# Opening of a pooling mixer and gated ConvFFN kernel: scale rows loaded and spread in four pieces, matmuls and averages of the first two tiles in another order, edge rows on another DMA queue

## The chip, the cores and the metric

The kernel runs on one core of one Trainium2 chip. The metric is device microseconds of the whole execution, as the median of three runs. All times below are in microseconds (us).

## What is computed

One layer of a decoder trunk: RMS norm, a causal pooling mixer with four windows, a residual, a second RMS norm, a gated ConvFFN (1024 to 2 x 2816 and back), a residual. The input is 1 x 1024 x 1024 in float32.

```python
h = rms_norm(x, norm_mix_g)
# pool_mixer: four groups of 256 channels, windows 2, 4, 8, 16
    groups.append(window_sum / count - xf[..., group])
d = jnp.stack(groups, axis=2)
y = einsum('bsgc,gcd->bsgd', d, w).reshape(bsz, seq, D_MODEL) + b
x = x + scale * y
f = conv_ffn(rms_norm(x, norm_ffn_g), ffn_w_in, ffn_conv_w, ffn_conv_b, ffn_w_out)
x = x + f
```

## The kernel before

The 1024 rows are cut into eight tiles `x0` to `x7` of 128 rows. For each tile the mixer makes these steps. `stat(j)` takes the mean square of a row (ScalarE, Square with a running sum, then Sqrt) and VectorE makes a factor of it. `mixer_norm(j)` multiplies the pooling band by that factor (VectorE, tile `bandr`). `mixer_window(j)` applies the band (TensorE, PSUM `psd`), and ScalarE copies the result to `dh`. `mixer_out(j)` multiplies by the pool weights (TensorE, PSUM `psy`, then two matmuls that add the bias rows), and VectorE adds the residual. `ffn_operand` transposes (PSUM `pst`) for the ConvFFN, whose two large products (names `X`, `Y`, `Z` and `oP`) fill the rest of the program after the first 60 us.

Ahead of that stands a short opening. Seven matmuls on a tile of zeros (`keep_warm`, L130) run while the first loads are on their way. The row of output scales (`rows`, 4 KB) is loaded into partition 0 of `rows_raw`, whose other 127 partitions are zeroed first by two memsets (L107 on VectorE, L108 on GpSimd). Two matmuls with a matrix of ones (`scale_rows`, L195) then spread that row to all partitions in PSUM `ps_scale`, and eight VectorE steps (`mixer_weights`, L200) multiply it and the norm's gain into the pool weights `wps`. `gain_rows` (L221) spreads the second norm's gain in the same way with the identity matrix, `pool_bias` prepares the bias rows. The last 16 rows of each tile are needed by the next one: they are loaded once for all tiles as `x_edge`, normed into `edge_band` (`edge_norm`) and multiplied in `mixer_edges` (PSUM `ps_edges`).

Each engine runs its instructions in order. That order is the order of the code with the constraints of `tc.issue_after`, which keep a block from being placed before a marked instruction. Loads stand in order on the queue of the engine that issues them: SyncE (SP) for nearly all, ScalarE for the scale row, GpSimd (POOL) for the eight-partition copy of the rows. PSUM for the mixer has three double banks (`bank2`) which the tiles `idle_ps`, `psd`, `ps_gain`, `psy`, `ps_edges`, `pst` take in turn.

Of the kernel before, what the change touches and what calls it, by code (L numbers as in the profile page):

```python
# [7 lines left out]
F32 = mybir.dt.float32  # L8
# [3 lines left out]
ALU = mybir.AluOpType  # L12
PSUM = bass.MemoryType.PSUM

P = 128
# [6 lines left out]
NG = 4  # L22
GRP = D // NG
WINDOWS = (2, 4, 8, 16)
HALO = 16
# [10 lines left out]
E0 = FAC + 2 * NG * HALO  # L36
# [7 lines left out]
NH = 512  # L44
# [4 lines left out]
def trunk_kernel(ctx: ExitStack, tc: tile.TileContext, x, consts, par, rows, pool_w, w_in, w_out, out):  # L49
    nc = tc.nc  # L50
# [11 lines left out]
    pp = pre.enter_context(tc.tile_pool(name="pre", bufs=1))  # L62
    ps_p = pre.enter_context(tc.tile_pool(name="ps_p", bufs=3, space=PSUM))

    def bank2(name):
        return ps_p.tile([P, 2 * NH], F32, tag="ps", name=name)

    def raw_tile(name):
        return work.tile([P, 2, D], F32, tag="raw", name=name, bufs=2)
# [15 lines left out]
    def load_x(j):  # L85
        if j < 2 or j >= 2 + XBUFS:
            xs[j] = hls.tile([P, D], F32, tag="hl", name=f"x{j}", bufs=7)
        else:
            xs[j] = pp.tile([P, D], F32, tag="x", name=f"x{j}", bufs=XBUFS)
        nc.sync.dma_start(xs[j], x[j * P : (j + 1) * P, :])  # L90

    cst = pp.tile([P, BD], F32, tag="cst", name="cst")
    band = pp.tile([P, NG, P], F32, tag="band", name="band")
    x_edge = work.tile([P, D], F32, tag="ha", name="x_edge", bufs=1)
    edge_band = work.tile([P, NG, P], F32, tag="sum", name="edge_band", bufs=3)
    def affine(t, src, op, fill, base, pattern, step):
        nc.gpsimd.affine_select(out=t, in_=src, compare_op=op, fill=fill, base=base, pattern=pattern, channel_multiplier=step)

    rows_raw = raw_tile("rows_raw")
    scale = rows_raw[:, 0, :]  # L100
    rows8, bias8 = (rows_raw[:NK, 1, i * NH : i * NH + 2 * P].rearrange("k (r p) -> k r p", p=P) for i in range(2))
    bias8 = bias8.bitcast(F32R)
    idle = work.tile([P, NH], BF16, tag="sum", name="idle", bufs=3)
    nc.vector.memset(idle, 0.0)
    eps_t = const.tile([P, 1], F32, tag="eps", name="eps_t")
    nc.vector.memset(eps_t, D * EPS)
    nc.vector.memset(scale[:, :NH], 0.0)  # L107
    nc.gpsimd.memset(scale[:, NH:], 0.0)  # L108
    warm = pp.tile([P, 1], F32, tag="warm", name="warm")
    with tc.issue_after(nc.scalar.dma_start(scale[:1, :], rows[:1, :]).ins):  # L110
        nc.scalar.activation(warm, eps_t, AF.Sqrt)

    nc.gpsimd.dma_start(rows8, rows.rearrange("r (k p) -> k r p", p=P))
    bias_hl = pp.tile([P, D], F32R, tag="bias_hl", name="bias_hl")
    nc.gpsimd.memset(bias_hl.bitcast(F32), 0.0)
    for g, w in enumerate(WINDOWS):
# [17 lines left out]
    nc.sync.dma_start(cst[:, :E0], consts[:, :E0])  # L134
    load_x(1)
    nc.sync.dma_start(par_sb[:, GM:], par[:, GM:])
    for g in range(0, NG, 2):
        nc.sync.dma_start(wp_raw[:, 2 * g : 2 * g + 4, :], pool_w[g : g + 2].rearrange("g (k p) d -> p (g k) d", p=P))
    nc.sync.dma_start(cst[:, E0:], consts[:, E0:])

    nc.sync.dma_start(x_edge, x.rearrange("(j r) d -> r j d", r=P)[P - HALO :, :, :])
    load_x(2)

    band0 = cst[:, :FAC].bitcast(BF16).rearrange("p (g s) -> p g s", s=P)
    fac = cst[:, FAC:E0].rearrange("p (c t) -> p c t", t=HALO)
# [3 lines left out]
    marks = {}  # L149

    def rstd_of(src, name):
        junk = pp.tile([P, D], BF16, tag="junk", name=f"junk_{name}")
        st = pp.tile([P, 4], F32, tag="st", name=f"st_{name}", bufs=8)
        nc.scalar.activation(junk, src, AF.Square, accum_out=st[:, 0:1])
        marks[name] = nc.scalar.activation(st[:, 1:2], st[:, 0:1], AF.Sqrt, bias=eps_t).ins
        nc.vector.tensor_scalar(st[:, 0:1], st[:, 0:1], D * EPS, None, op0=ALU.add)

        nc.vector.scalar_tensor_tensor(st[:, 3:4], st[:, 1:2], st[:, 1:2], st[:, 0:1], op0=ALU.mult, op1=ALU.add)
        nc.vector.reciprocal(st[:, 2:3], st[:, 3:4])
        return st[:, 1:2], st[:, 2:3]  # L160

    def normed(out, src, r):
        return nc.vector.tensor_scalar(out, src, r[0], r[1], op0=ALU.mult, op1=ALU.mult).ins
# [3 lines left out]
    def edge_norm():  # L167
        marks["edge"] = normed(edge_band, band_e, rstd_of(x_edge, "e"))

    def mixer_norm(j):  # L170
        t = bands[j] = pp.tile([P, NG, P], F32, tag="bandr", name=f"bandr{j}", bufs=2)
        marks[f"band{j}"] = normed(t, band if j else band0, stats[j])

    def windows(ps, src, weights):
        for c in range(NK):
            m = nc.tensor.matmul(ps[:, c * P : (c + 1) * P], src[:, c * P : (c + 1) * P], weights[:, c // 2, :], start=True, stop=True)  # L176
        return m.ins

    ones = pp.tile([P, P], F32R, tag="ones", name="ones")
# [3 lines left out]
    def mixer_edges():  # L183
        ps = marks["ps_edges"] = bank2("ps_edges")
        marks["edges_pe"] = windows(ps, x_edge, edge_band)
        first_edges()
        marks["edges"] = nc.scalar.activation(edges, ps.rearrange("p (c s) -> p c s", c=NK), AF.Copy).ins


    wps = pp.tile([P, 2 * NG, GRP], F32, tag="wps", name="wps")  # L190
    def scale_rows():

        ps = [ps_x.tile([P, NH], F32, tag="X", name=f"ps_scale{h}") for h in range(2)]
        for h in range(2):
            marks["scale"] = nc.tensor.matmul(ps[h], ones.bitcast(F32), scale[:, h * NH : (h + 1) * NH], start=True, stop=True).ins  # L195
        return [ps[g // 2][:, g % 2 * GRP : (g % 2 + 1) * GRP] for g in range(NG)]

    def mixer_weights(scale_b, chunks):
        for c in chunks:
            marks["wps"] = nc.vector.scalar_tensor_tensor(  # L200
                wps[:, c, :], scale_b[c // 2], par_sb[:, GM + c : GM + c + 1], wp_raw[:, c, :], op0=ALU.mult, op1=ALU.mult
            ).ins
# [14 lines left out]
    def gain_rows():  # L217
        ps = bank2("ps_gain")
        for k in range(NK):
            gain = par_sb[:, GF + k : GF + k + 1].to_broadcast([P, P])  # L220
            marks["gain_pe"] = nc.tensor.matmul(ps[:, k * P : (k + 1) * P], gain, ident, start=True, stop=True).ins  # L221
        gain_b = pp.tile([P, D], F32, tag="gain_b", name="gain_b")
        marks["gain"] = nc.scalar.activation(gain_b, ps, AF.Copy, scale=FOLD).ins
        return gain_b

    ds, gains = {}, []

    def mixer_window(j):
        ps = bank2(f"psd{j}")
        marks[f"psd{j}"] = windows(ps, xs[j], bands.pop(j))  # L230
        dh = ds[j] = pp.tile([P, NK, P], F32, tag="dh", name=f"dh{j}", bufs=2)
        ps3 = ps.rearrange("p (c s) -> p c s", c=NK)
        first = ps3[:, :, :HALO]
        if j == 0:
            marks["first"] = nc.vector.tensor_tensor(first, first, fac, ALU.mult).ins
        elif j > 1:
            nc.vector.tensor_tensor(first, first, edges[:, :, j * HALO : (j + 1) * HALO], ALU.add)
        marks[f"dh{j}"] = nc.scalar.activation(dh, ps3, AF.Copy).ins
# [208 lines left out]
    def stat(j):  # L447
        if j in xs and j not in stats:
            stats[j] = rstd_of(xs[j], f"a{j}")

    scale_b = scale_rows()
    stat(0)
    mixer_norm(0)
    with tc.issue_after(marks["band0"]):
        nc.vector.tensor_tensor(b8, b8, rows8[:, 0, :], ALU.mult)
        stat(1)
        mixer_norm(1)
    with tc.issue_after(marks["scale"]), tc.issue_after(marks["band1"]), tc.issue_after(marks["a1"]):
        mixer_window(0)
    with tc.issue_after(marks["dh0"]), tc.issue_after(marks["first"]):  # L460
        pool_bias()
    with tc.issue_after(marks["first"]):
        mixer_weights(scale_b, range(2 * NG))
    with tc.issue_after(marks["psd0"]), tc.issue_after(marks["dh0"]):
        mixer_window(1)
    with tc.issue_after(marks["dh1"]), tc.issue_after(marks["wps"]):
        edge_norm()
    with tc.issue_after(marks["e"]), tc.issue_after(marks["edge"]):
        stat(2)
        mixer_norm(2)  # L470
    with tc.issue_after(marks["psd1"]), tc.issue_after(marks["a2"]):
        gains.append(gain_rows())
    with tc.issue_after(marks["gain_pe"]), tc.issue_after(marks["band2"]):
        mixer_out(0, stats=False)
    with tc.issue_after(marks["psy0"]):
        mixer_edges()
    with tc.issue_after(marks["dh1+"]), tc.issue_after(marks["gain"]):
        stat(3)
        mixer_norm(3)
    with tc.issue_after(marks["band3"]), tc.issue_after(marks["edges"]):  # L480
        mixer_out_stats(0)
# [180 lines left out]
    for k in range(-SLOOK, len(oevents)):  # L662
# [9 lines left out]
        with tc.issue_after(lasts[-1]) if lasts else nullcontext():  # L672
            room = 4
            if k + OLOOK < len(oevents):
                e = oevents[k + OLOOK]
# [19 lines left out]
        if f == 0 and opens:  # L695
            for i in range(4):
                tag = ("XXYY" if set_ == "X" else "YZZZ")[i]
# [14 lines left out]
        for i, g, c, bank in steps:  # L712
            a, b = oops[p, g]
            alone = opens and (p, i) != ("P4", 3)
            for m, (u, v) in enumerate(((0, 0), (0, 1), (1, 0))):
                first = g == (NP2 - TAIL if c.start else 0) and m == 0
                nc.tensor.matmul(  # L717
                    bank, a[:, u, i * P : (i + 1) * P], b[:, v, c],
                    start=opens and first, stop=g == NP2 - 1 and m == 2, skip_group_check=not alone,
# [82 lines left out]
```

## Time and profile before

| | us |
|---|---|
| median of three runs | 701.74 (701.55 to 701.88) |
| the profiled execution | 702.16 |
| its span, first to last instruction | 700.3 |
| TensorE busy in it | 692.7 (99%) |
| VectorE busy | 598.9 (86%) |
| ScalarE busy | 343.3 (49%) |
| GpSimd busy | 13.2 (2%) |

The profile lists, for each engine, when an instruction started, how long it took and what ended the idle time before it. The chain of waits follows the work that ended last back to the start: what stands in it sets the end of the program.

### The profile page before, as it was taken

Reading aid. Unit: us, or ns where it says so; the run is one execution under the profiler, and the core shown is the slowest. Engines: PE = TensorE matmul, PEld = TensorE weight load, DVE = VectorE, ACT = ScalarE, POOL = GpSimd, SP = SyncE. Lnnn points to the kernel's source line nnn. Section 1 sums busy time; section 2 is a strip of 40 time slices with the busy share of each in tenths; the row PEclk is TensorE's granted clock in tenths of the full one; section 3 lists DMA queues with packets and bytes.
Section 4 is the critical chain, followed back from the end, with each engine's and each line's share of the span. In section 5 each row is a group of like instructions: output and inputs, shape, how many; then the busy total and the mean of one; then the engine's idle time right before and its main releaser. Section 6 shows DMA issues by size and latency. Waiting matters only on the chain.

```text
span 700.3 us, 8502 instructions
## 1 busy us (share of the span) xinstructions
PE 692.7 (99%) x3160; PEld 574.4 (82%) x3160; DVE 598.9 (86%) x884; ACT 343.3 (49%) x515; POOL 13.2 (2%) x31
## 2 busy tenths in 40 slices
PE   8999999999999999999999999999999999999998
PEld 5998778888888888888888888888888888888886
DVE  4788999999888888888988888876887988999985
ACT  5786645454444454444445454454554344444431
POOL 3021000000000000000000000000000000000000
PEclk9999999999999999999999999999999999999999
DMA  8974112222122112222222212229989700122131
GB/s 243 318 175 136 61 60 91 100 111 91 77 74 85 52 75 90 91 90 91 91 90 91 90 61 91 94 84 345 321 312 347 266 23 0 61 90 89 62 107 61
DMA packets 32556, 85.49 MB, mean 122 GB/s; under 512 B 3689, under 2 KB 5377, under 8 KB 29698
## 3 DMA queue, kind: packets, MB, share of 16 engines
q1 hardware_dynamic: 31328, 82.83, 33.4%
q0 software_dynamic: 1184, 2.11, 1.7%
q8 instruction: 25, 0.41, 0.2%
q14 instruction: 17, 0.14, 0.1%
q10 hardware_dynamic: 2, 0.00, 0.0%
HBM read 62.89 MB, written 19.92 MB: 118 GB/s over the span
## 4 chain that ended last, share of the span: by engine, by line
PE 97%; DVE 1%; DMA 1%; ACT 0%; issue 0%; DVEq 0%; ACTq 0%
PE oP L717 30%; PE Y L366 26%; PE Z L366 17%; PE X L366 16%; PE psy L253 4%; PE psd L176 2%; PE pst L286 1%; DMA rows_raw<-in_rows_dram 1%; PE psy L256 1%; PE ps_scale L195 0%; DVE n2f L317 0%; DVE T L306 0%; PE ps_gain L221 0%; PE ps_edges L176 0%; DVE n L271 0%; DVE S4s L77 0%
## 5 line engine op out<-in xcount | busy, mean ns | idle before, releaser
L717 PE MATMUL oP<-oBP,oAP 128*128 128x512 f32 (+1 forms) x924 | 208.8, 388 | 0.0
L717 PEld LDWEIGHTS oP<-oBP,oAP 128*128 128x128 f32 x924 | 172.9, 188 | 36.0 <-DVE oBP L77 0.3
L366 PE MATMUL Z<-T,S1s 128*128 128x512 f32 x264 | 64.1, 390 | 1.4 <-ACT T L305 1.2
L366 PE MATMUL X<-B,A11s 128*128 128x512 f32 x264 | 64.3, 390 | 0.0
L366 PE MATMUL Y<-T,S2s 128*128 128x512 f32 x264 | 64.0, 390 | 0.0
L366 PE MATMUL X<-B,A12s 128*128 128x512 f32 x264 | 63.5, 389 | 0.0
L366 PE MATMUL Y<-T,S3s 128*128 128x512 f32 x264 | 63.4, 389 | 0.0
L366 PE MATMUL Y<-T,A22s 128*128 128x512 f32 x264 | 63.4, 389 | 0.0
L366 PE MATMUL Z<-B,S4s 128*128 128x512 f32 x264 | 63.2, 389 | 0.0
L366 PEld LDWEIGHTS Z<-T,S1s 128*128 128x128 f32 x264 | 49.3, 188 | 12.6 <-ACT T L305 1.6
L366 PEld LDWEIGHTS Y<-T,S2s 128*128 128x128 f32 x264 | 49.4, 188 | 10.8 <-ACT S2s L76 0.4
L366 PEld LDWEIGHTS Y<-T,S3s 128*128 128x128 f32 x264 | 49.5, 188 | 10.3
L366 PEld LDWEIGHTS Y<-T,A22s 128*128 128x128 f32 x264 | 49.6, 188 | 10.3
L366 PEld LDWEIGHTS Z<-B,S4s 128*128 128x128 f32 x264 | 49.5, 188 | 10.3
L366 PEld LDWEIGHTS X<-B,A12s 128*128 128x128 f32 x264 | 49.5, 188 | 10.2
L366 PEld LDWEIGHTS X<-B,A11s 128*128 128x128 f32 x264 | 49.4, 188 | 10.2
L76 ACT ACTIVATE oBP<-blk 128x512 fp32r<-128x512 f32 x53 | 33.5, 633 | 49.1 <-PE oP L717 33.6
L77 DVE TENSOR_TENSOR oBP<-blk,oBP 128x512 fp32r<-128x512 f32 x53 | 36.7, 692 | 13.3 <-ACT oBP L76 13.3
L424 ACT ACTIVATE gate<-gate 128x1024 f32<-128x1024 f32 x22 | 23.3, 1061 | 44.5 <-DVE gate L415 44.5
L76 ACT ACTIVATE oAP<-blk 128x512 fp32r<-128x512 f32 x55 | 34.1, 621 | 19.2 <-DVE blk L317 15.9
L320 DVE TENSOR_TENSOR win<-win 128x512 f32<-128x512 f32 x60 | 41.3, 689 | 1.1
L77 DVE TENSOR_TENSOR oAP<-blk,oAP 128x512 fp32r<-128x512 f32 x55 | 37.8, 687 | 2.6 <-ACT oAP L76 2.6
(128 smaller groups left out, 940.8 us busy)
## 6 DMA issues: line engine op xcount, KB each, us to landing
win<-in_w_in_dram SPq DMA_DIRECT2D x22, 1024.0 KB, 4.8
g_dram<-val SPq DMA_DIRECT2D x22, 512.0 KB, 2.6
blk<-g_dram SPq DMA_DIRECT2D x33, 256.0 KB, 5.3
blk<-in_w_out_dram SPq DMA_DIRECT2D x31, 256.0 KB, 5.8
A12s<-g_dram SPq DMA_DIRECT2D x22, 256.0 KB, 5.2
B21s<-in_w_out_dram SPq DMA_DIRECT2D x22, 256.0 KB, 2.7
x<-in_x_dram SPq DMA_DIRECT2D x8, 512.0 KB, 4.9
x_dram<-x SPq DMA_DIRECT2D x8, 512.0 KB, 3.0
```

The costliest lines, as they stand in the source:

```text
L76: nc.scalar.activation(t[:, 0, :], src, AF.Copy)
L77: m = nc.vector.tensor_tensor(t[:, 1, :], src, t[:, 0, :].bitcast(F32), ALU.subtract)
L176: m = nc.tensor.matmul(ps[:, c * P : (c + 1) * P], src[:, c * P : (c + 1) * P], weights[:, c // 2, :], start=True, stop=True)
L253: nc.tensor.matmul(o, dh[:, c, :], wps[:, c, :], start=c % 4 == 0, stop=False, skip_group_check=True)
L256: m = nc.tensor.matmul(ps[:, cols], ones, bias_hl[:, cols], start=False, stop=True, skip_group_check=True)
L286: nc.tensor.transpose(ps[:, c * P : (c + 1) * P], n2[:, c * P : (c + 1) * P], ident)
L320: nc.vector.tensor_tensor(out, a, b, ALU.add)
L366: nc.tensor.matmul(bank, a[:, i, ks], b[:, l, k, :], start=opens and m == 0, stop=m == 11, skip_group_check=not opens)
L424: nc.scalar.activation(gate, gate, AF.Silu)
L717: nc.tensor.matmul(bank, a[:, u, i * P : (i + 1) * P], b[:, v, c], start=opens and first, stop=g == NP2 - 1 and m == 2, skip_group_check=n ...
```

## The change

The scale row goes as four pieces of 256 into four partitions of a tile with 256 columns; one VectorE memset zeroes these columns. A new tile `pick` (128 x 4, ones on its diagonal, made by GpSimd) takes the place of the matrix of ones: column g, stretched over 128 columns, selects row g, so there are four matmuls of 256 columns where two of 512 stood. The memset of the zeros for `keep_warm` goes from VectorE to GpSimd. On SP's queue the second part of the constants (identity and edge band) goes ahead of the pool weights, and `x_edge` leaves it for GpSimd's queue, so `x2` follows the pool weights. `gain_rows` goes between the windows of tiles 0 and 1, `stat(2)` ahead of the copy of tile 1, `edge_norm` behind it.

```diff
-    scale = rows_raw[:, 0, :]
+    scale = rows_raw[:, 0, :GRP]
...
-    nc.vector.memset(idle, 0.0)
+    nc.gpsimd.memset(idle, 0.0)
+    nc.vector.memset(scale, 0.0)
...
-    nc.vector.memset(scale[:, :NH], 0.0)
-    nc.gpsimd.memset(scale[:, NH:], 0.0)
...
-    with tc.issue_after(nc.scalar.dma_start(scale[:1, :], rows[:1, :]).ins):
+    with tc.issue_after(nc.scalar.dma_start(scale[:NG, :], rows[0].rearrange("(g d) -> g d", d=GRP)).ins):
...
+    pick = pp.tile([P, NG], F32, tag="pick", name="pick")
+    nc.gpsimd.memset(pick, 0.0)
+    affine(pick, pick, ALU.not_equal, 1.0, 0, [[1, NG]], -1)
...
+    nc.sync.dma_start(cst[:, E0:], consts[:, E0:])
     for g in range(0, NG, 2):
         nc.sync.dma_start(wp_raw[:, 2 * g : 2 * g + 4, :], pool_w[g : g + 2].rearrange("g (k p) d -> p (g k) d", p=P))
-    nc.sync.dma_start(cst[:, E0:], consts[:, E0:])
-
-    nc.sync.dma_start(x_edge, x.rearrange("(j r) d -> r j d", r=P)[P - HALO :, :, :])
     load_x(2)
+
+    nc.gpsimd.dma_start(x_edge, x.rearrange("(j r) d -> r j d", r=P)[P - HALO :, :, :])
...
-        for h in range(2):
-            marks["scale"] = nc.tensor.matmul(ps[h], ones.bitcast(F32), scale[:, h * NH : (h + 1) * NH], start=True, stop=True).ins
+        for g in range(NG):
+            marks["scale"] = nc.tensor.matmul(rows_b[g], pick[:, g : g + 1].to_broadcast([P, P]), scale, start=True, stop=True).ins
...
-    with tc.issue_after(marks["scale"]), tc.issue_after(marks["band1"]), tc.issue_after(marks["a1"]):
+    with tc.issue_after(marks["scale"]), tc.issue_after(marks["a1"]):
         mixer_window(0)
+    with tc.issue_after(marks["first"]):
+        mixer_norm(1)
...
+    with tc.issue_after(marks["psd0"]), tc.issue_after(marks["bias"]):
+        gains.append(gain_rows())
+    with tc.issue_after(marks["gain"]), tc.issue_after(marks["wps"]):
         stat(2)
         mixer_norm(2)
...
+    with tc.issue_after(marks["gain_pe"]), tc.issue_after(marks["a2"]):
+        mixer_window(1)
+    with tc.issue_after(marks["dh1"]), tc.issue_after(marks["band2"]):
+        edge_norm()
+    with tc.issue_after(marks["psd1"]), tc.issue_after(marks["edge"]):
         mixer_out(0, stats=False)
```

On TensorE, from the spreading of the scale rows to the edges (`psd0`, `psd1` and `psd2` are the windows of tiles 0, 1 and 2). First before, then now:

```order
L195 MATMUL ps_scale0_175<-rows_raw_85,ones_144 128x512
L195 MATMUL ps_scale1_176<-rows_raw_85,ones_144 128x512
L176 MATMUL psd0_198<-bandr0_186,x0_132 128x128 x8
L176 MATMUL psd1_233<-bandr1_196,x1_135 128x128 x8
L221 MATMUL ps_gain_261<-cst_81,par_sb_122 128x128 x8
L253 MATMUL psy0_272<-wps_147,dh0_207 128x256 x8
L256 MATMUL psy0_272<-bias_hl_96,ones_144 128x512 x2
L176 MATMUL ps_edges_285<-edge_band_84,x_edge_83 128x128 x8
```

```order
L199 MATMUL ps_scale0_179<-rows_raw_85,pick_95 128x256 x2
L199 MATMUL ps_scale1_180<-rows_raw_85,pick_95 128x256 x2
L179 MATMUL psd0_202<-bandr0_192,x0_136 128x128 x8
L225 MATMUL ps_gain_239<-cst_81,par_sb_126 128x128 x8
L179 MATMUL psd1_259<-bandr1_214,x1_139 128x128 x8
L257 MATMUL psy0_278<-wps_151,dh0_211 128x256 x8
L260 MATMUL psy0_278<-bias_hl_100,ones_148 128x512 x2
L179 MATMUL ps_edges_298<-edge_band_84,x_edge_83 128x128 x8
```

The gain matmuls have moved one place ahead, between the windows; the number of matmuls up to the edges is the same but for the four of 256 columns. Behind the edges the order of every engine is as it was.

On ScalarE, from the copy of tile 0 to the mean square of tile 3 (`a2`, `a3` and `e` are the mean squares of `x2`, `x3` and of the edge rows). First before, then now:

```order
L238 ACTIVATE dh0_207<-psd0_198 128x1024
L208 ACTIVATE rows_raw_85<-rows_raw_85 8x128
L238 ACTIVATE dh1_242<-psd1_233 128x1024
L154 ACTIVATE junk_e_244,st_e_245<-x_edge_83 128x1024
L155 ACTIVATE st_e_245<-st_e_245,eps_t_88 128x1
L154 ACTIVATE junk_a2_252,st_a2_253<-x2_142 128x1024
L155 ACTIVATE st_a2_253<-st_a2_253,eps_t_88 128x1
L223 ACTIVATE gain_b_270<-ps_gain_261 128x1024
L154 ACTIVATE junk_a3_296,st_a3_297<-x3_214 128x1024
```

```order
L242 ACTIVATE dh0_211<-psd0_202 128x1024
L212 ACTIVATE rows_raw_85<-rows_raw_85 8x128
L227 ACTIVATE gain_b_248<-ps_gain_239 128x1024
L157 ACTIVATE junk_a2_250,st_a2_251<-x2_145 128x1024
L158 ACTIVATE st_a2_251<-st_a2_251,eps_t_89 128x1
L242 ACTIVATE dh1_268<-psd1_259 128x1024
L157 ACTIVATE junk_e_270,st_e_271<-x_edge_83 128x1024
L158 ACTIVATE st_e_271<-st_e_271,eps_t_89 128x1
L157 ACTIVATE junk_a3_291,st_a3_292<-x3_221 128x1024
```

The copy of the gain rows and the mean square of `x2`, which stood behind that of the edge rows, now stand ahead of it and of the copy of tile 1.

On SP's queue, the first loads (the `x` with the lowest number is `x0`, the next `x1`, the last `x2`). First before, then now:

```order
L90 DMA x_132<-in_x_dram 128x1024
L134 DMA cst<-in_consts_dram 128x384
L90 DMA x_135<-in_x_dram 128x1024
L136 DMA par_sb<-in_par_dram 128x16
L138 DMA wp_raw<-in_pool_w_dram 128x4x256 x2
L139 DMA cst<-in_consts_dram 128x384
L141 DMA x_edge<-in_x_dram 128x1x1024
L90 DMA x_142<-in_x_dram 128x1024
```

```order
L90 DMA x_136<-in_x_dram 128x1024
L137 DMA cst<-in_consts_dram 128x384
L90 DMA x_139<-in_x_dram 128x1024
L139 DMA par_sb<-in_par_dram 128x16
L140 DMA cst<-in_consts_dram 128x384
L142 DMA wp_raw<-in_pool_w_dram 128x4x256 x2
L90 DMA x_145<-in_x_dram 128x1024
```

`x2` has the place that `x_edge` had; `x_edge` is now the last of GpSimd's opening work, behind its twelve selects for the bands and two instructions for `pick`.

## Rows read from the trace of the kernel before

**Rows 1.** The page: busy time, share of the span and instructions of each engine.
```profile
PE 692.7 (99%) x3160; PEld 574.4 (82%) x3160; DVE 598.9 (86%) x884; ACT 343.3 (49%) x515; POOL 13.2 (2%) x31
```

**Rows 2.** The chain of waits, first 85 us: start, duration, what stood in it.
```profile
1.84 4.01 DMA rows_raw<-in_rows_dram
...
5.99 3.41 PE ps_scale L195 x4
9.39 3.57 PE psd L176 x32
12.97 1.79 PE ps_gain L221 x16
14.75 3.46 PE psy L253 x16
...
18.67 1.78 PE ps_edges L176 x16
...
65.73 0.89 PE pst L286 x8
```

**Rows 3.** Timeline of TensorE at the start: start, duration, instruction, idle time before it.
```profile
1.26 3.17 PE L130 MATMUL idle_ps<-idle 128*128 128x512 bf16 x7 [1.26 <-DVE idle L104]
5.99 3.41 PE L195 MATMUL ps_scale<-rows_raw,ones 128*128 128x512 f32 x4 [1.56 <-DMA rows_raw<-in_rows_dram]
```

**Rows 4.** Timeline of VectorE in the opening, columns as in Rows 3.
```profile
0.93 0.27 DVE L104 MEMSET idle<- 128x256 uint32 x1 [0.93 <-PEq L793]
...
1.26 0.48 DVE L107 MEMSET rows_raw<- 128x512 f32 x1
...
11.22 0.30 DVE L235 TENSOR_TENSOR psd<-psd,cst 128x128 f32<-128x128 f32 x1 [1.01 <-PE psd L176]
...
13.01 2.03 DVE L200 SCALAR_TENSOR_TENSOR wps<-ps_scale,par_sb,wp_raw 128x256 f32<-128x256 f32 x5
...
16.84 0.55 DVE L163 TENSOR_SCALAR edge_band<-cst,st_e 128x512 f32<-128x512 bf16 x1
```

**Rows 5.** DMA issues of the first 5 us, one load each: size, us from issue to landing.
```profile
x<-in_x_dram SPq DMA_DIRECT2D x1, 512.0 KB, 3.3
...
rows_raw<-in_rows_dram POOLq DMA_DIRECT2D x1, 8.0 KB, 5.3
...
par_sb<-in_par_dram SPq DMA_DIRECT2D x1, 8.0 KB, 5.4
```

**Rows 6.** Timeline of GpSimd: the last of its opening work, columns as in Rows 3.
```profile
5.26 1.72 POOL L97 TENSOR_SCALAR_AFFINE_SELECT band<-band 128x128 f32<-128x128 f32 x6
```

**Rows 7.** DMA issues around 4.3 to 5 us, columns as in Rows 5.
```profile
x_edge<-in_x_dram SPq DMA_DIRECT2D x1, 512.0 KB, 10.2
cst<-in_consts_dram SPq DMA_DIRECT2D x1, 192.0 KB, 8.5
```

**Rows 8.** Timeline of ScalarE from the copy of tile 0 on, columns as in Rows 3.
```profile
11.55 1.02 ACT L238 ACTIVATE dh<-psd 128x1024 f32<-128x1024 f32 x1 [2.64 <-DVE psd L235]
12.47 0.29 ACT L208 ACTIVATE rows_raw<-rows_raw 8x128 fp32r<-8x128 f32 x1
13.00 1.02 ACT L238 ACTIVATE dh<-psd 128x1024 f32<-128x1024 f32 x1 [0.24 <-PE psd L176]
14.68 1.06 ACT L154 ACTIVATE junk_e<-x_edge 128x1024 bf16<-128x1024 f32 x1 [0.66 <-DMA x_edge<-in_x_dram]
...
16.07 1.04 ACT L154 ACTIVATE junk_a<-x 128x1024 bf16<-128x1024 f32 x1
...
17.43 1.01 ACT L223 ACTIVATE gain_b<-ps_gain 128x1024 f32<-128x1024 f32 x1
```

**Rows 9.** Stretches: busy of PE, PEld, DVE, ACT, POOL, clock, DMA share, GB/s.
```profile
2.00:3.00 1.00, 1.00 (x4) 0.36 (x3) 0.00 (x0) 0.62 (x1) 1.00 (x2) 1.00 1.01 332
...
10.00:11.00 1.00, 1.00 (x11) 1.00 (x10) 0.21 (x1) 0.00 (x0) 0.00 (x0) 1.00 0.99 161
...
12.00:13.00 1.00, 1.00 (x11) 1.00 (x10) 0.89 (x3) 0.76 (x2) 0.00 (x0) 1.00 1.10 254
```

More of the change, by code (lines that the diff above doesn't have):

```diff
@@ L193, in scale_rows @@
         ps = [ps_x.tile([P, NH], F32, tag="X", name=f"ps_scale{h}") for h in range(2)]
-        for h in range(2):
-            marks["scale"] = nc.tensor.matmul(ps[h], ones.bitcast(F32), scale[:, h * NH : (h + 1) * NH], start=True, stop=True).ins
-        return [ps[g // 2][:, g % 2 * GRP : (g % 2 + 1) * GRP] for g in range(NG)]
+        rows_b = [ps[g // 2][:, g % 2 * GRP : (g % 2 + 1) * GRP] for g in range(NG)]
+        for g in range(NG):
+            marks["scale"] = nc.tensor.matmul(rows_b[g], pick[:, g : g + 1].to_broadcast([P, P]), scale, start=True, stop=True).ins
+        return rows_b
     def mixer_weights(scale_b, chunks):
@@ L456, in trunk_kernel @@
         stat(1)
+    with tc.issue_after(marks["scale"]), tc.issue_after(marks["a1"]):
+        mixer_window(0)
+    with tc.issue_after(marks["first"]):
         mixer_norm(1)
-    with tc.issue_after(marks["scale"]), tc.issue_after(marks["band1"]), tc.issue_after(marks["a1"]):
-        mixer_window(0)
-    with tc.issue_after(marks["dh0"]), tc.issue_after(marks["first"]):
+    with tc.issue_after(marks["band1"]):
+        mixer_weights(scale_b, range(1))
+    with tc.issue_after(marks["dh0"]), tc.issue_after(marks["wps"]):
         pool_bias()
[L462 to L468, printed above, removed]
+    with tc.issue_after(marks["bias_dve"]):
+        mixer_weights(scale_b, range(1, 2 * NG))
+    with tc.issue_after(marks["psd0"]), tc.issue_after(marks["bias"]):
+        gains.append(gain_rows())
+    with tc.issue_after(marks["gain"]), tc.issue_after(marks["wps"]):
         stat(2)
         mixer_norm(2)
-    with tc.issue_after(marks["psd1"]), tc.issue_after(marks["a2"]):
-        gains.append(gain_rows())
-    with tc.issue_after(marks["gain_pe"]), tc.issue_after(marks["band2"]):
+    with tc.issue_after(marks["gain_pe"]), tc.issue_after(marks["a2"]):
[3 more added lines that the diff above has]
+    with tc.issue_after(marks["psd1"]), tc.issue_after(marks["edge"]):
         mixer_out(0, stats=False)
-    with tc.issue_after(marks["psy0"]):
+    with tc.issue_after(marks["e"]):
+        stat(3)
+    with tc.issue_after(marks["psy0"]), tc.issue_after(marks["a3"]):
         mixer_edges()
-    with tc.issue_after(marks["dh1+"]), tc.issue_after(marks["gain"]):
-        stat(3)
+    with tc.issue_after(marks["dh1+"]):
         mixer_norm(3)
```

## The prediction

> **What bounds the kernel now.** The page comes first: TensorE is busy for 692.7 us of a span of 700.3 [rows 1], so only 7.6 us of the span is not TensorE's, and an edit gains time only where TensorE waits. Next the chain of waits. It starts with the load of the scale row (1.84, 4.01 us long), and from 5.99 on it is TensorE without a break until 65.73 + 0.89: scale rows, two windows, gain rows, `psy`, edges [rows 2]. TensorE's timeline agrees: the seven matmuls on zeros end at 4.43, and the scale matmuls wait 1.56 us for the row [rows 3]. So what counts is the time at which TensorE gets through the opening. I take the start of the edge matmuls as the mark, 18.67 [rows 2]: behind it each engine keeps its order, TensorE's work is the same, and the chain hangs on TensorE, so a shift of that start is a shift of the end. I call it T, and s is the start of the scale matmuls (5.99 before).
>
> **The scale row.** Its load waits for the memsets. VectorE's memset of 512 columns runs from 1.26 to 1.74 behind that of the zeros, which has 256 columns of 32 bits and takes 0.27 from 0.93 [rows 4]. Now the only memset ahead of the load is one of 256 such columns, from 0.93 to 1.20: 0.54 us sooner. If the load again takes 4.01 us from its issue, s = 5.99 - 0.54 = 5.45. Bounds: `x0`, the quickest load there, takes 3.3 us, which gives s = 4.74; if the row is served at the same time as before however early it is asked for, s = 5.99; the slow small loads of that time take 5.3 and 5.4, which gives 6.8 [rows 5]. I take 5.45, since the same queue, bytes and neighbours are closest to the same row. Four matmuls of 256 columns stream as many columns as two of 512: 3.41 us [rows 2], no change. `pick` is made by GpSimd before the first band select, whose last selects end at 6.98 [rows 6], 1.72 us for six; twelve selects and their memsets come behind it, so it is there well before 5. The zeros' memset on GpSimd may delay the warm-up matmuls by some tenths; the 1.56 us gap behind them covers that [rows 3].
>
> **TensorE's demand.** From s the work is a fixed sum [rows 2]: scale 3.41, a window 3.57/2 = 1.79, gain 1.79, a window 1.79, then `psy` with its bias, 18.67 - 14.75 = 3.92. So the gain rows end at s + 6.98, `psy` starts at s + 8.76, and the edges are asked for at s + 12.68, which is 18.13 with s = 5.45. That gains 0.54 if everything else is ready. The moved gain rows need the identity, which landed at 3.70 + 8.5 = 12.2 before [rows 7] and now goes ahead of 1 MB of pool weights, asked for at s + 5.2 = 10.65: ready. The factors of tile 1 now follow VectorE's step on the first columns of `psd0`; that step starts at 11.22, s + 5.23 [rows 4], so 0.30 + 0.55 later, s + 6.1, against s + 6.98: covered with 0.9 us. The pool weights: seven of eight VectorE steps wait for ScalarE's copy of the bias (s + 6.5 + 0.29) [rows 8]; at 2.03/5 = 0.41 each [rows 4] the last ends at about s + 10, where `psy`, taking 3.46/8 = 0.43 per weight [rows 2], asks for it at s + 11.8: covered.
>
> **The new wait.** The edges need `edge_band`, and that hangs on ScalarE's order. Before, its mean square began at 14.68, and `edge_band` was done at 16.84 + 0.55 = 17.39 [rows 4, 8]: 2.71 us later, and 1.28 before TensorE asked. Now ScalarE does the copy of the gain rows, the mean square of `x2` and the copy of tile 1 first. Prices from starts to starts [rows 8]: a copy 12.47 - 11.55 = 0.92, a mean square 17.43 - 16.07 = 1.36. The gain copy starts 0.03 behind TensorE's last gain matmul, as the copy of tile 1 did (13.00 against 12.97) [rows 2, 8], at s + 7.01; `x2` at s + 7.93; tile 1 at s + 9.29; the edges at s + 10.21; `edge_band` ends at s + 12.92, the matmul starts 0.04 later, s + 12.96. That is 0.28 behind TensorE's demand: of the 0.54 gained 0.26 is left, T = 18.41.
>
> But `x2` must have landed at s + 7.93 = 13.38, else every 0.1 us of lateness is 0.1 on T: T = landing + 1.36 + 0.92 + 2.71 + 0.04 = landing + 5.03. Where does it land? It takes the place of `x_edge` in SP's queue, with the same bytes ahead, and `x_edge` landed at 4.43 + 10.2 = 14.63 [rows 7]. The strided edge rows were slow: with the DMA engines fully busy, 161 to 254 GB/s flowed from 10 to 13, against 332 when `x0` flowed [rows 9]. 0.52 MB at the middle, 208, takes 2.52; at 332 it takes 1.58: `x2` would land 0.94 sooner, at 13.69. **Sum:** T = 18.72, which is 0.05 later than 18.67. Bounds: `x2` before 13.38 gives -0.26; no quicker than the edge rows, 14.63, gives T = 19.66, +0.99. If s stays 5.99, T is at least 18.95, +0.28, within these. The sum is made against the profiled execution, 702.16 (span 700.3 and 1.86 around it), which would become 702.2; the median of the runs, 701.74, lies 0.42 lower and becomes 701.8.
>
> A rule that speaks against the move of the edge rows to GpSimd: the Trainium skill, "Trainium Kernel Development and Optimization", Key Constraints, says that DMAs issued from SP, ScalarE and GpSimd run on the same 16 DMA engines and interleave, so that issuing from several engines saves only the issue time. The trace agrees as far as it goes (the 8 KB load on GpSimd's queue took 5.3 us beside SP's loads) [rows 5], but it has no long transfer on two queues at once. By that rule `x2` and `x_edge` would share the engines, and the time would be that of rival 2.
>
> **Rivals.** 1. *TensorE's clock rises sooner, and `x2` comes early: faster.* The profile gives the granted clock as 1.00 in every stretch, but a scale matmul streams at half rate: 3.41 us for 2 x 512 columns, against 3.46 for 8 x 256 in `psy` [rows 2]. That is the lower level, 1.2 GHz, and the windows behind it run at 2.4. Before the rise TensorE had worked 3.17 us, idled 1.56 and worked 3.41 [rows 3]. With a gap of about 1.0 the rise might come in the scale matmuls, which then cost up to 3.41/2 = 1.71 less. For it: the gap shrinks. Against it: even then `x2` and the edge rows decide. `x2` stands behind constants and weights of which the last landed at 12.2 [rows 7]; at 12.2 T is 17.23, -1.44. With 12.2 to 13 the time is 700.3 to 701.1, middle 700.7. Since that landing was itself slowed by the edge rows, half of this case lies beyond 0.2%.
>
> 2. *`x2` and the edge rows share the DMA engines: slower.* GpSimd issues `x_edge` behind its selects, at about 7.4 (6.98 and `pick`) [rows 6]; the small load on that queue took 5.3 to land [rows 5], so the edge rows land at 12.7 at the earliest and move while `x2` does. If both finish together, `x2` lands with the last byte: before, that was between 14.63 and 16.07, where ScalarE took `x2` without a wait [rows 7, 8]. ScalarE stands there with the copy of tile 1 and the edges queued behind it, VectorE and TensorE wait for them. At 15.2, T = 20.23, +1.56: 703.3; at 16.07, +2.43: 704.2. It decides from a landing of 13.64 (no gain) and passes 0.2% at 15.04. The edge rows themselves give the same: landed later than `x2` + 2.28 they hold the same step; at 7.4 + 10.2 = 17.6, +1.7.
>
> 3. *The load starts sooner but lands no sooner* (s = 5.99): the change doesn't do what it says, T = 18.95, 702.0.
>
> **How the numbers follow.** Forecast 701.8, own range 701.5 to 702.7: chance 0.45. Rival 1, 700.7: 0.23. Rival 2, 703.3: 0.24. Rival 3, 702.0: 0.08. What a measurement of this kernel can tell from no change is about 0.2%, 1.4 us: faster than 700.34 is half of rival 1, 0.12; slower than 703.14 is two thirds of rival 2 and a little, 0.17; within it 0.71. The range reaches down to rival 1's middle less a little, 700.4, and up to 703.5 in rival 2, leaving out about 1 in 10 on each side.
>
> **What would show it.** Right: the load of the scale row issued at 1.3, scale matmuls at about 5.45; the gain rows between two windows without a wait; ScalarE waiting for `x2` until about 13.7; TensorE waiting for `edge_band` some tenths, edges at about 18.7, and from there the old timeline. Wrong: scale matmuls at 1.7 us in all (rival 1); ScalarE waiting for `x2` or the edge rows past 15 (rival 2); the row landing at 5.85 again (rival 3); or a wait behind the edges that the profile before does not have, which would break the rule that a shift of T is a shift of the end.

## The result, and the profile after

The changed kernel takes 704.48 us (median of 7 runs, 702.92 to 705.45); the kernel before took 701.53 beside it (7 runs, 701.03 to 701.88). The ratio is 1.0039, 95% interval 1.0029 to 1.0049: slower by 0.4%, outside the predicted range of 700.4 to 703.5. The runs of the changed kernel fall into two groups by their mean granted clock: four with 0.997 take 704.48 to 705.45 (mean 704.89), three with 0.999 or 1.00 take 702.92 to 703.49 (mean 703.12). The profiled execution is one of the first group: 705.0 us, span 702.9, clock 0.997, against 702.16, 700.3 and 1.00 before. The mean of the second group, 703.12, lies within the range.

The page's line of busy times, to be set beside [rows 1]: TensorE has four matmuls more, as the diff says, and is busy 1.2 us longer.

```profile
PE 693.9 (99%) x3164; PEld 576.7 (82%) x3164; DVE 598.3 (85%) x883; ACT 343.2 (49%) x515; POOL 14.0 (2%) x34
```

The chain of waits of the changed kernel (start us, us, what stood in it), to be set beside [rows 2]:

```profile
0.81 3.44 DMA x<-in_x_dram
4.25 0.02 issue
4.27 9.95 DMA x<-in_x_dram
14.22 0.02 issue
14.24 1.16 ACT junk_a L157 x2
...
15.71 0.91 ACT dh L242
16.63 1.04 ACT junk_e L157 x2
...
19.31 3.47 PE ps_edges L179 x16
22.79 1.96 PE psd L179 x16
24.75 3.46 PE psy L257 x16
...
489.68 208.71 PE oP L725 x924
```

Before, the chain was TensorE's from 5.99 on. Now it starts with loads (the first row is `x0`, the row from 4.27 to 14.22 is `x2`), goes through ScalarE (mean square of `x2`, copy of tile 1, mean square of the edges) and reaches TensorE only at 19.31. The last row is the long run of `oP` matmuls near the end. Before it read `487.21 208.69`: it starts 2.47 us later now and is as long as it was, so all that the change cost happened ahead of it.

TensorE's timeline at the start (start, duration, instruction, idle time before it and what ended that), to be set beside [rows 3]:

```profile
1.38 3.17 PE L133 MATMUL idle_ps<-idle 128*128 128x512 bf16 x7 [1.38 <-POOL idle L104]
4.34 2.69 PE L199 MATMUL ps_scale<-rows_raw,pick 128*128 128x256 f32 x8
7.08 2.05 PE L179 MATMUL psd<-bandr,x 128*128 128x128 f32 x16
8.97 1.95 PE L225 MATMUL ps_gain<-cst,par_sb 128*128 128x128 f32 x16
10.76 1.95 PE L179 MATMUL psd<-bandr,x 128*128 128x128 f32 x16
12.54 3.62 PE L257 MATMUL psy<-wps,dh 128*128 128x256 f32 x16
15.81 0.82 PE L260 MATMUL psy<-bias_hl,ones 128*128 128x512 f32 x2
19.31 3.47 PE L179 MATMUL ps_edges<-edge_band,x_edge 128*128 128x128 f32 x16 [2.68 <-ACT junk_a L157]
```

Up to the edges the rows are better than forecast: the wait of 1.56 us for the scale row is gone, the view lists no idle time from 4.34 to 16.6, and TensorE is ready for the edges two microseconds sooner than before. Then it idles 2.68 us, and the 16 edge matmuls take 3.47 us where they took 1.78 [rows 2]. The idle time is named by its last releaser; the chain above shows what it hangs on.

ScalarE's timeline in the same stretch, to be set beside [rows 8]:

```profile
1.23 0.55 ACTq L109 DMA_DIRECT2D rows_raw<-in_rows_dram  x1
...
11.07 1.00 ACT L227 ACTIVATE gain_b<-ps_gain 128x1024 f32<-128x1024 f32 x1
14.24 1.06 ACT L157 ACTIVATE junk_a<-x 128x1024 bf16<-128x1024 f32 x1 [2.17 <-DMA x<-in_x_dram]
...
15.62 1.00 ACT L242 ACTIVATE dh<-psd 128x1024 f32<-128x1024 f32 x1
16.53 1.04 ACT L157 ACTIVATE junk_e<-x_edge 128x1024 bf16<-128x1024 f32 x1
```

And the row of VectorE's timeline that ends this, beside the last of [rows 4]:

```profile
18.66 0.55 DVE L166 TENSOR_SCALAR edge_band<-cst,st_e 128x512 f32<-128x512 bf16 x1
```

ScalarE waits 2.17 us for `x2`; copy, edge statistics and `edge_band` stand behind it. Last, TensorE's granted clock in the stretches around the edges (length, busy of PE, PEld, DVE, ACT, POOL, clock, DMA share, GB/s):

```profile
18.00:20.00 2.00, 0.69 (x4) 0.72 (x5) 1.87 (x5) 1.32 (x3) 0.00 (x0) 0.90 0.98 391
20.00:22.00 2.00, 2.00 (x12) 2.00 (x11) 0.34 (x1) 0.00 (x0) 0.00 (x0) 0.50 1.03 405
22.00:25.00 3.00, 3.00 (x22) 2.97 (x22) 1.43 (x6) 1.85 (x2) 0.00 (x0) 0.83 0.87 287
```

In the kernel before all three read 1.00; its middle one:

```profile
20.00:22.00 2.00, 2.00 (x21) 2.00 (x20) 1.28 (x5) 1.18 (x2) 0.00 (x0) 1.00 0.97 324
```

Between 20 and 22 the clock of the changed kernel is at its lower level, 1.2 GHz, behind the idle time; by 25 it is back. It does not fall in the idle time itself: it reads 1.00 from 19.4 to 19.6, when the edge matmuls have begun, and 0.50 from 19.8 to 20.0. The clock lost is 2 x 0.10 + 2 x 0.50 + 3 x 0.17 = 1.71 us. So the 2.47 come out as: edges started later than before (19.31 against 18.67) 0.64, edges slower 3.47 - 1.78 = 1.69, the window behind them 1.96 - 1.79 = 0.17, together 2.50. What lies around the span (the time of the execution less its span) grew from 1.86 to 2.1.

### The profile page after: what moved, and what is told of

Same layout as the page of the kernel before. It is cut to its first block, busy times and chain, and to the rows that moved or that the text cites. A ratio compares the mean times of both kernels' runs of the same rounds, so it can differ in the third digit from the quotient of the medians.

```text
span 702.9 us, 8512 instructions
## 1 busy us (share of the span) xinstructions
PE 693.9 (99%) x3164; PEld 576.7 (82%) x3164; DVE 598.3 (85%) x883; ACT 343.2 (49%) x515; POOL 14.0 (2%) x34
## 4 chain that ended last, share of the span: by engine, by line
PE 95%; DMA 2%; DVE 1%; ACT 1%; issue 0%; DVEq 0%
PE oP L725 30%; PE Y L370 26%; PE Z L370 17%; PE X L370 16%; PE psy L257 3%; DMA x<-in_x_dram 2%; PE psd L179 2%; PE pst L290 1%; PE ps_edges L179 0%; DVE n2f L321 0%; PE psy L260 0%; ACT junk_a L157 0%; DVE T L310 0%; DVE n L275 0%; DVE S4s L77 0%; PE rest L725 0%
```

## The experiments

Theory A: the idle time ahead of the edges makes the clock fall, and this is what the forecast lacked. Theory B: the loss lies in later transfers or later work (the edges start late for `x2`), and the clock is an accident of one profiled run. Further rivals were that one half of the change (the scale row, the order) costs by itself, and that the edge rows on GpSimd's queue hold up `x2`. All runs are set against runs of the kernel before that were taken beside them; its row counts the 58 beside the experiments. A run is called fallen where its mean clock is 0.997 or 0.998. T is the start of the edge matmuls in the chain, oP the start of the `oP` row.

| kernel | median us | ratio to before, 95% | runs at clock 0.999 or 1.00: mean | runs at 0.997 or 0.998: mean | T | oP | oP - T |
|---|---|---|---|---|---|---|---|
| before | 701.53 to 701.89 | 1 | 56: 701.82 | 2: 702.76, 703.69 | 18.67 | 487.21 | 468.54 |
| after | 704.48 | 1.0039 (1.0029 to 1.0049) | 3: 703.12 | 4: 704.89 | 19.31 | 489.68 | 470.37 |
| e4_fill | 703.20 | 1.0018 (1.0009 to 1.0026) | 11: 703.19 | none | 19.27 | 487.88 | 468.61 |
| e1_edges_first | 701.79 | 1.0002 (0.9992 to 1.0012) | 10: 701.61 | 2: 704.26 | 17.83 | 486.59 | 468.76 |
| e5_scale_only | 701.37 | 0.9995 (0.9986 to 1.0003) | 11: 701.50 | none | 18.24 | 486.81 | 468.57 |
| e6_order_only | 704.59 | 1.0032 (1.0020 to 1.0045) | 2: 702.80 | 4: 704.70 | 19.23 | 488.01 | 468.78 |
| e7_sp_behind | 702.64 | 1.0015 (1.0003 to 1.0027) | 8: 702.44 | 4: 704.50 | 18.79 | 489.22 | 470.43 |
| e2_edges_first_sp | 700.89 | 0.9987 (0.9978 to 0.9995) | 11: 700.94 | none | 16.68 | 485.40 | 468.72 |
| e8_edges_between | 700.85 | 0.9987 (0.9978 to 0.9995) | 11: 700.98 | none | 17.54 | 486.22 | 468.68 |

The last column says most. In the seven profiled executions whose clock stayed up, the way from T to `oP` is 468.5 to 468.8 us whatever was changed ahead of T; the 0.2 among them is the edge matmuls' 2.02 for 1.78 where a wait stands ahead of them. In the two whose clock fell it is 470.4. Two of the 56 runs of the kernel before, 703.73 and 703.80, are as late as a fallen run with the clock at 1.00; they have no profile, so a late run is not always one whose clock fell.

**Matmuls in the gap.** The changed kernel, with twelve matmuls on zeros between `psy` and the edges, whose result nobody reads:

```
-    with tc.issue_after(marks["psy0"]), tc.issue_after(marks["a3"]):
+    fill_ps = ps_x.tile([P, NH], F32, tag="X", name="fill_ps")
+    with tc.issue_after(marks["psy0"]):
+        for _ in range(12):
+            marks["fill"] = nc.tensor.matmul(fill_ps, idle[:, :P], idle, start=True, stop=True).ins
+    with tc.issue_after(marks["fill"]), tc.issue_after(marks["a3"]):
```

> The changed kernel plus twelve matmuls on zeros (128x512 bf16, result unused, 0.22 us each at full rate) between the bias matmuls of psy0 and the edge matmuls, so that TensorE works where it idled 2.7 us. Theory A (late edge band, then a lower TensorE clock): the edges still start at about 19.3, but take 1.78 instead of 3.47 us and the window behind them 1.79 instead of 1.96; the time falls by about 1.9 to 702.6, and its spread over runs (702.9 to 705.5 before) shrinks to a few tenths. Theory B (the loss lies in later transfers or later work): the time stays at 704 to 705.

Measured: 703.20, and in none of 11 runs did the clock fall. TensorE's timeline:

```profile
16.51 2.76 PE L487 MATMUL fill_ps<-idle 128*128 128x512 bf16 x12
19.11 1.95 PE L179 MATMUL ps_edges<-edge_band,x_edge 128*128 128x128 f32 x16
```

The same place and `oP` in the chain of waits:

```profile
16.67 2.60 PE fill_ps L487 x12
19.27 1.78 PE ps_edges L179 x16
...
487.88 208.71 PE oP L729 x924
```

The edges start 0.04 us from where they started without the filling and take 1.78 again; `oP` starts 1.80 sooner. Work that does nothing but keep TensorE busy gives back what the clock took: A, against B. The forecast of the size was too good: the median falls by 1.28 and not by 1.9, because three of the changed kernel's seven runs had no fall to give back (against its four fallen runs it is 1.70), and the runs still spread over 1.2 us. The rest of the loss stays. (In this run `x2` landed by 13.38, so the edges could have started at about 18.4; here the filling itself was the last to end.)

**The scale row alone.** The kernel before, with the changed scale load, `pick`, memsets and scale matmuls, and the old order:

```
-    scale = rows_raw[:, 0, :]
+    scale = rows_raw[:, 0, :GRP]
...
+            marks["scale"] = nc.tensor.matmul(rows_b[g], pick[:, g : g + 1].to_broadcast([P, P]), scale, start=True, stop=True).ins
```

> The kernel before with the scale row alone changed (four pieces, pick, memsets), loads and order as before. Theory A: scale matmuls at 4.3, the clock rises in them, so psd0 ends at 8.9; psd1 waits for its band until 10.3, the gain rows for the identity until 12.2, the edges for edge_band: x_edge lands at 14.6, so edges at about 17.4 to 18.0 against 18.67. 700.3 to 700.9. A rival, that the early start is worth nothing because the loads decide: 701.5.

Measured: 701.37, ratio 0.9995, not told apart from no change; mean 701.50 against 701.83 for the runs of before with the clock up. TensorE's timeline:

```profile
4.43 2.25 PE L199 MATMUL ps_scale<-rows_raw,pick 128*128 128x256 f32 x8
6.91 2.05 PE L179 MATMUL psd<-bandr,x 128*128 128x128 f32 x16 [0.23 <-DVE bandr L166]
10.01 2.05 PE L179 MATMUL psd<-bandr,x 128*128 128x128 f32 x16 [1.04 <-DVE bandr L166]
12.29 2.02 PE L225 MATMUL ps_gain<-cst,par_sb 128*128 128x128 f32 x16 [0.24 <-DMA cst<-in_consts_dram]
```

The scale matmuls start 1.56 us sooner and end 2.7 sooner, and all but 0.4 of it is waited away again: 0.23 + 1.04 for the bands, 0.24 for the identity, which lands at 12.2 here as before, and three times some 0.25 more, since 16 matmuls behind a wait take 2.02 to 2.05 and not 1.79. The 700.3 to 700.9 expected were missed; the rival's 701.5 came true. This half of the change is harmless, and its gain is small because TensorE's next operands aren't ready.

**The order alone.** The changed kernel with the scale row loaded and spread as before (`scale = rows_raw[:, 0, :]` and two matmuls of 512 columns against `ones`).

> The changed kernel with the scale row as before (one row of 1024, ones, two memsets), so only loads and order are changed. Theory A: scale matmuls at 5.99 at the lower clock as before; edge_band hangs on x2 (14.2 + 5.03 = 19.25), edges at 19.3; TensorE idles about 0.6 us and its clock stays: +0.6, 702.1. That would say that the loss needs both halves: the order makes the edges late, the early start makes the idle time long. A rival, that the order alone costs it all: 704 to 705.

Measured: 704.59; four of six runs with a fallen clock. I had expected 702.1; the rival's 704 to 705 came true. The profiled execution is one of the two with the clock up; TensorE's timeline of it:

```profile
5.02 3.75 PE L195 MATMUL ps_scale<-rows_raw,ones 128*128 128x512 f32 x4 [0.60 <-DMA rows_raw<-in_rows_dram]
...
19.23 2.02 PE L176 MATMUL ps_edges<-edge_band,x_edge 128*128 128x128 f32 x16 [0.90 <-ACT junk_a L154]
```

With 0.90 us idle the clock held in this run; the four that fell have no profile, so how long they idled, and that they fell at the edges, is not shown. The order is what costs, in both ways: 1.0 by the later edges (702.80 against 701.83), and 1.9 more where the clock falls.

**The edges first on ScalarE.** The changed kernel, with the copy of tile 1 and the edges' mean square moved ahead of the mean square of `x2`:

```
+    with tc.issue_after(marks["gain_pe"]), tc.issue_after(marks["gain"]):
+        mixer_window(1)
+    with tc.issue_after(marks["dh1"]), tc.issue_after(marks["wps"]):
+        edge_norm()
+    with tc.issue_after(marks["e"]), tc.issue_after(marks["edge"]):
+        stat(2)
+        mixer_norm(2)
...
```

> The changed kernel with one thing undone: the copy of tile 1 and the mean square of the edge rows stand ahead of the mean square of x2 again; queues as in the changed kernel. Theory A: the edge rows landed at 7.13 + 7.9 = 15.03, so their mean square starts there, edge_band ends at about 17.75, the edges start at 17.8 (19.31 in the changed kernel, 18.67 in the one before); TensorE idles 1.3 us. If the clock stays up, 700.7; if it falls as it does in the changed kernel, 702.5. Theory B: 704 to 705.

Measured: 701.79; ten runs with a mean of 701.61, two with a fallen clock at 704.16 and 704.37. ScalarE's timeline:

```profile
15.03 1.06 ACT L157 ACTIVATE junk_e<-x_edge 128x1024 bf16<-128x1024 f32 x1 [1.42 <-DMA x_edge<-in_x_dram]
```

TensorE's:

```profile
17.83 2.02 PE L179 MATMUL ps_edges<-edge_band,x_edge 128*128 128x128 f32 x16 [1.35 <-ACT junk_a L157]
```

That one exchange takes back the loss of the whole change. The edges start where expected, but the runs with the clock up lie 0.9 above the 700.7 expected: 0.24 of that is the edge matmuls' 2.02 for 1.78, some 0.2 lies around the span, the rest is not explained. What is late now is the landing of the edge rows, which GpSimd issued at about 7.2; 1.35 us of idle time are left in the profiled run, and the clock fell in two runs of twelve.

**The edge rows on SP's queue behind `x2`.** The order of the changed kernel, with one line different:

```
-    nc.gpsimd.dma_start(x_edge, ...)
+    nc.sync.dma_start(x_edge, ...)
```

> The changed kernel with one thing undone: x_edge goes on SP's queue, behind x2; the order on ScalarE stays, x2 ahead of tile 1 and the edge rows. If the edge rows on GpSimd's queue are what delays x2 (rival 2 of the prediction: both share the DMA engines), x2 lands at about 13.4 or sooner instead of 14.2, edges at 18.4, TensorE idles less, 701 to 703 by the clock. If x2's place behind the pool weights sets its landing, it lands at 14.2 as before and the time stays at 704 to 705. The microseconds outside the span, 2.0 in the kernels with x_edge on GpSimd against 1.8 before, would be 1.8 again if the GpSimd queue is their cause.

Measured: 702.64; eight runs with a mean of 702.44, four fallen with 704.50. The profiled run is a fallen one: TensorE's timeline:

```profile
18.79 2.92 PE L179 MATMUL ps_edges<-edge_band,x_edge 128*128 128x128 f32 x16 [2.18 <-ACT junk_a L157]
21.50 2.73 PE L179 MATMUL psd<-bandr,x 128*128 128x128 f32 x16
```

The stretch with the edges, columns as above:

```profile
20.00:22.00 2.00, 2.00 (x11) 2.00 (x11) 0.26 (x2) 0.00 (x0) 0.00 (x0) 0.50 1.04 369
```

Taking the transfer off GpSimd cures neither the idle time nor the clock. Without the fall it is 0.7 better than after (702.44 against 703.12), which would fit an `x2` that lands sooner: 13.69 here, 14.22 in after. But with the rows on GpSimd's queue `x2` landed at 14.22 (after), 14.14 (order alone) and by 13.38 (gap filled), one run each, so whether the second queue delays `x2` is not settled.

**Both: edges first, and their rows on SP ahead of `x2`.** The reordering of "The edges first on ScalarE", with the `x_edge` load on SP between the pool weights and `x2`.

> Kernel e1_edges_first (edge rows ahead of x2 on ScalarE) with x_edge on SP's queue ahead of x2, as before the change. The edge rows landed at 15.03 by GpSimd's queue and at 14.63 or 14.2 by SP's: edges at 17.0 to 17.4 instead of 17.83, TensorE idles 0.6 to 1.0 and its clock stays: 700.0 to 700.6. If the queue makes no difference, 701.8 with some runs at 704 as e1.

Measured: 700.89, ratio 0.9987 with its interval below 1, and no fallen clock in 11 runs. ScalarE's timeline:

```profile
13.87 1.06 ACT L157 ACTIVATE junk_e<-x_edge 128x1024 bf16<-128x1024 f32 x1
```

TensorE's:

```profile
16.68 2.02 PE L179 MATMUL ps_edges<-edge_band,x_edge 128*128 128x128 f32 x16
```

The rows are there by 13.87, against 15.03 by GpSimd's queue, the edges follow `psy` with 0.06 us between, and `oP` starts 1.81 sooner than before. This is the version that beats both kernels, by 0.75 us against before (700.89 against 701.64 beside it). The 700.0 to 700.6 expected were missed, although the edges start sooner than expected. The 1.81 is the difference of two single executions, of which this one (700.33) is faster than its kernel's median and the one before (702.16) slower, so it overstates the gain.

**The edge rows between the two pool-weight loads.** The last kernel with the load one place further forward.

> Kernel e2_edges_first_sp with x_edge between the two loads of the pool weights. If the landing of the edge rows is what holds TensorE, it comes at about 13.2, edge_band ends at 16.3 and TensorE asks for the edges at 16.46: no idle time, edges at about 16.5, 699.4 to 699.8. If the second half of the pool weights is late instead (landing past 14.3), TensorE waits in psy0 and the gain is smaller by that wait.

Measured: 700.85, the same as with the rows behind both loads; the second of the two expectations came true. The price of the place shows in VectorE's timeline:

```profile
14.55 1.66 DVE L205 SCALAR_TENSOR_TENSOR wps<-ps_scale,par_sb,wp_raw 128x256 f32<-128x256 f32 x4 [1.56 <-DMA wp_raw<-in_pool_w_dram]
```

And in TensorE's:

```profile
15.09 1.99 PE L258 MATMUL psy<-wps,dh 128*128 128x256 f32 x8 [0.56 <-DVE wps L205]
```

The second half of the pool weights is late and `psy` waits 0.56 for it. The profiled execution is the slowest of its 11 runs (701.70), so it shows the wait and not its mean cost.

## Why the prediction was wrong

**The step that failed: "a shift of that start is a shift of the end".** T came out at 19.31, 0.64 later than before, inside the forecast's own bounds (18.41 to 19.66). By the rule the profiled run would be 702.16 + 0.64 = 702.8; it was 705.0. The rule holds wherever the clock stays up (468.5 to 468.8 in seven profiles) and fails by 1.8 where TensorE has idled long ahead of T. The prediction priced idle time at its length and nothing more. It had used the clock itself in rival 1, for a gain at the start, and not asked the same of the gap ahead of the edges. Among its signs of being wrong it did name a break of this rule, but as a wait behind the edges; there is none, the matmuls themselves are slower. Filling the gap took the 1.8 away: shown. The Trainium skill, "TensorE: Matmul & The Clock Gate", section "HAM oscillation — how this bites in real kernels", tells of a kernel in which the array waits about 3 to 5 us for a load between groups of matmuls, is throttled again and starts the next group cold. The trace agrees in part: 0.50 granted in 20 to 22, behind the wait; but here waits of 2.68 and 2.18 us stood ahead of the fall, and the edge matmuls began with the clock still at 1.00.

**The start was too good, in both its terms.** s came out at 4.34, under the lower bound of 4.74: the row was there within 3.1 us of its issue at 1.23, where the sum had 4.01 and its quickest neighbour 3.3 [rows 5]. The scale matmuls took 2.69 in place of 3.41, so by their durations the clock rose in them, the mechanism of rival 1. TensorE therefore asked for the edges at 16.6, against a forecast of 18.13. Rival 1 expected a gain only if `x2` came early too; it came at 14.22, so the 1.5 us gained became idle time. The order-alone run, which keeps the late start, lost as much, so the early start is not needed for the loss.

**`x2`: right mechanism, size off.** Landing 14.22 for 13.69, inside the bounds. The formula for T stands: landing + 5.03 gives 19.25 for 19.31 here, 18.72 for 18.79 and 19.17 for 19.23 in the two other runs where `x2` decided. So ScalarE's order, priced by rows of before, was right to 0.07 us. Rival 2's price needed a landing of 15.2 and did not occur; that its 703.3 is nearer to the result is chance. By the rule of the Trainium skill that the prediction weighed ("Trainium Kernel Development and Optimization", Key Constraints) `x2` and the edge rows run on the same DMA engines and interleave. The trace agrees: from 11 to 13, with `x2` not yet landed, the engines moved 0.36 MB for GpSimd's queue, on which only the edge rows were left, and 0.10 MB for SP's. What that cost `x2` is open: it landed at 13.69 with the edge rows behind it on SP's queue, and by 13.38 in one run with them on GpSimd's.

**Where the prediction saw no difficulty and there was none.** The gain rows between the two windows, the identity, the pool weights and the factors of tile 1 show no wait; `pick` was made by 3.5; `oP` took as long as before. Rival 3 fell: the row landed sooner.

**What stays open.** First, about 0.2 us around the span: it is 1.93 to 2.01, as the mean of the runs, in every kernel with the new order, also with the edge rows on SP, against 1.78 to 1.80 in before and 1.75 in the scale-only kernel. Second, with the clock up after lies 1.70 above before (703.12 against 701.42, the mean of the seven runs), or 1.30 above the 56 runs of the table; T (0.64), the span's surroundings (0.2) and edge matmuls at 2.02 for 1.78 (0.24, as in the order-alone run) give 1.1. They are read from single executions, and the profiled one of before, 702.16, is slower than both means. Third, what length of idle time decides: the clock fell in profiles with 2.18 and 2.68 and held with 0.90 and 1.35, but kernels of the latter kind also fell in some runs, three of the seven runs of after did not, and two of 58 of before did, which shows no gap ahead of the edges in its profile.

## What to carry to other kernels

Price an idle stretch of TensorE twice: its length, and what the matmuls behind it cost if the clock falls, here 1.7 to 1.9 us behind a gap of 2.2 to 2.7 in two profiles (the means of fallen and other runs of one kernel lie 1.8 to 2.7 apart). When the work ahead of a gap is made faster and the operand behind it doesn't come sooner, the gap grows, so look first for what will be late next: here one exchange on ScalarE and one place in SP's queue took 3.6 us off the changed kernel's median, while the new scale row alone is not told apart from no change. Where a kernel's runs fall into two groups, read the granted clock of each run before explaining their median.

## What was not expected of the hardware

The granted clock does not show the half rate of the opening. The seven matmuls on zeros took 3.17 us, 0.45 each, and the twelve of the same form in the gap 2.60, 0.22 each; yet the stretch from 0 to 5 of the changed kernel reads 1.00:

```profile
0.00:5.00 5.00, 3.62 (x9) 1.69 (x10) 0.42 (x3) 2.21 (x3) 4.23 (x17) 1.00 0.61 185
```

By these durations the rise comes at another moment in each run: with the same four-piece scale row and starts of 4.34 to 4.43, the eight scale matmuls took 1.92, 1.96, 2.25, 2.47, 2.64, 2.69 and 2.77 us. And the 4 KB row took at most 3.1 to 3.2 us from its issue to its first user in these runs, also in the order-alone kernel, where it is issued at 1.84 as before: beside these, the 4.15 of the one profile before (4.01 to its landing) looks like a late case, and the bound taken from its neighbours was too high.
